# Taking GpSimd's elementwise work in the attention stage over to VectorE and ScalarE

## The chip, the cores and the metric

The kernel runs on one core of one Trainium2 chip. The metric is the device time of one execution in microseconds (us). Engines are named as in the profile: PE is TensorE's matmul and PEld its weight load, DVE is VectorE, ACT is ScalarE, POOL is GpSimd, SP is SyncE, which issues the DMAs.

## The reference: what is computed

One encoder block over 512 tokens plus 16 meta tokens, model width 1024, float32. All heads are 64 wide.

```
u = rms_norm(h, pre_mix_gain)
qa, ka, va, qb, kb, vb, g = split(u @ w_in)            # 1024 -> 6656 columns
qa, ka, qb, kb = rope(...)                             # x1*cos - x2*sin, x2*cos + x1*sin
o_swa  = softmax([q k^T in a window of 3 blocks, 16 meta keys, sink]) v     # 16 heads, 4 KV heads
o_diff = (softmax(q1 k1^T) - lam * softmax(q2 k2^T)) v                      # 8 heads, all 528 keys
o_diff = rms_norm(o_diff, per head) * (1 - lambda_init)
merged = sigmoid(g1 + b1) * (o_swa @ w_branch_swa) + sigmoid(g2 + b2) * (o_diff @ w_branch_diff)
h = h + rms_norm(merged @ w_out)
h = h + rms_norm((silu(a) * b) @ w_ffn_out),  [a, b] = rms_norm(h) @ w_ffn_in
```

## The kernel before

Every float32 operand of a large product is split into a high part (a rounded copy, written by ACT) and a low part (the source minus the high part, `sub_hi`). A product is then three matmuls, hi·hi, hi·lo and lo·hi, which `mm3` (L142 to L144) accumulates in PSUM. All weights come as tiles of 128x1024 float32: `load_w` issues the DMA on SP's queue, ACT writes the high part `wh` (L130), and `sub_hi` (L111) writes the low part `wl`. For the 48 weight tiles from the 4th to the 51st (a counter `nw`), POOL writes three quarters of `wl` (128x768) and DVE the last quarter (128x256); for the others DVE writes all of it.

The order of PE's instructions is fixed when the kernel is built: several streams, written as generators, are merged by a class `Order`, in which each stream states how much PE time it just used and how long its next operands will take (the table `LAT`). The streams are the two halves of windowed attention (`s_swa` for scores and softmax, `t_swa` for transposes and values), the same two of differential attention (`s_diff`, `t_diff`), and `fill`, which puts projections (`f_q`, `f_qk`, `f_vd`, `f_gate`, `f_b1` and others) between them. The order on DVE, ACT, POOL and SP's queue in this stage is chosen by the framework's scheduler, and each engine works its list strictly as it stands. An instruction with a wait holds up what is behind it on its engine.

The places that the change touches, in the order of the work:

- Rotary embedding (`rope`): DVE multiplies the two PSUM tiles by the cosines and sines (L325, L326) into `ta` and `tb`, POOL adds them (L327), ACT and DVE split the sum into `hl` (L118, L119). DMAs rearrange `hl` into the operands of the score products.
- Windowed attention works in 16 units (4 KV heads by 4 query blocks), each of four heads. Per head: two score matmuls into `Sw` (L465), DVE adds the mask and takes the smallest value (L468), ACT takes the exponential and its sum (L471). The sink value is put into the column behind the keys by a POOL copy of one column (L467). When all four sums are there, DVE inverts them (`rc`, L474) and POOL scales the four heads' rows (L476). Then PE transposes them (L516), ACT and DVE split the transposes into `ah` and `al` (L115, L111), and PE multiplies them with V (L530, L531, and L534 for the meta keys out of `aTm`).
- Differential attention: 8 heads of 4 query blocks, two softmaxes each. Per softmax four matmuls into `Sd` (L626), which is one buffer of two banks, a DVE minimum `dnm` (L629) and an ACT exponential (L630). Then DVE inverts the sums (L634), multiplies one by minus lambda (L635), POOL scales the first softmax (L636) and DVE adds the second (L638).
- Per head, the RMS norm over 128 rows of the output: ACT squares, `split(sh, sl, sq, eng=pool)` has POOL write the low part, PE sums (L691), ACT forms `v` and `y` = v^-0.5 (L695 to L697), and a Newton step follows: POOL computes z = y·y, z·v and 1.5 - 0.5·z (L699 to L701), DVE multiplies y by z (L702) and by gain and output (L703).

Of the kernel before, what the change touches and what calls it, by code (L numbers as in the profile page):

```python
"""Hybrid encoder block: windowed GQA with sink + differential attention, gated merge, SwiGLU FFN.

Every float32 operand of a large product is split exactly into two float32r parts (hi + lo);
a product is hi*hi + hi*lo + lo*hi accumulated in float32 in PSUM.
"""
# [10 lines left out]
AF = mybir.ActivationFunctionType  # L16
ALU = mybir.AluOpType
# [3 lines left out]
P = 128  # L21
# [13 lines left out]
class Order:  # L35
    """Order in which the tensor engine takes the work of several streams.

    A stream is a generator; it yields (cost, delay): the tensor time just traced and how long after
    it the stream's next piece has its operands, or a function that tells when (None: not yet) the
    next piece may follow. The first stream that is ready goes on."""  # L40
# [55 lines left out]
def encoder(ctx, tc, I, out, dbg=None):  # L96
# [25 lines left out]
    nw = [0]  # L122

    def load_w(src, k=KT, dst=None):
        raw = wp.tile([P, k, D // k], F32, tag="wr", name="wr", bufs=RB)
        sp.dma_start(out=raw, in_=src.rearrange("p (k c) -> p k c", k=k))
        if dst is None:
            dst = [wp.tile([P, k, D // k], F32R, tag=t, name=t) for t in ("wh", "wl")]
        wh, wl = dst
        act.copy(out=wh, in_=raw)  # L130
        # during attention the vector engine is the busiest: GpSimd takes three quarters of the low parts
        nw[0] += 1
        cut = 3 * k // 4 if 4 <= nw[0] < 52 else 0
        if cut:
            sub_hi(wl[:, 0:cut], raw[:, 0:cut], wh[:, 0:cut], pool)
        sub_hi(wl[:, cut:], raw[:, cut:], wh[:, cut:])
        return wh, wl
# [18 lines left out]
    def rsqrt_cols(pl, ss, n, scale, tag, extra=None, bufs=1):  # L156
        """(ss*scale + eps)^-0.5 on [n, m] columns, with one Newton step; extra replaces eps."""
# [54 lines left out]
    # the tensor engine's clock rises only under load  # L212
# [59 lines left out]
    # K of the windowed branch, slice by slice as x arrives; then V  # L272
# [13 lines left out]
    # row statistics of x: 1/rms, broadcast to all partitions  # L286
# [28 lines left out]
    # small vectors  # L315
# [5 lines left out]
    def rope(hl, psa, psb, c0, n, o0, scale=None):  # L321
        """psa, psb: [P, n] products of columns c0..c0+n; hl[:, part, hi/lo, o0..o0+n] gets the rotated split."""
# [4 lines left out]
        pool.tensor_tensor(out=ta, in0=ta, in1=tb, op=ALU.add)  # L327
# [104 lines left out]
    # per query block: (key column range, mask, [(offset in range, key block or -1 for meta)])  # L432
# [10 lines left out]
    # meta rows of the transposed probabilities; the gaps between the row groups stay zero  # L443
# [4 lines left out]
    def s_swa():  # L448
        for u in range(16):
# [9 lines left out]
            pt = atp.tile([P, 4, 401], F32, tag="p", name="p", bufs=2)  # L459
            for hh in range(4):  # L460
# [6 lines left out]
                pool.tensor_copy(out=p[:, nk:nk + 1], in_=nsink[:, h:h + 1])  # L467
# [7 lines left out]
            for hh in range(4):  # L475
                pool.tensor_scalar(out=pt[:, hh, 0:nk], in0=pt[:, hh, 0:nk], scalar1=rc[:, hh:hh + 1],  # L476
                                   scalar2=1.0, op0=ALU.mult, op1=ALU.mult)
# [5 lines left out]
    def pipe(n, tr_fn, av_fn, done_tr, free_at):  # L483
        """tr_fn(k), then av_fn(k, operand): two transposed banks ahead."""
# [122 lines left out]
    def s_diff():  # L607
        for h in range(8):
# [8 lines left out]
            for i in range(4):  # L617
# [4 lines left out]
                for c in range(2):  # L622
                    S = ps.tile([P, 2, 512], F32, tag="S", name="Sd")
                    for s in range(2):
                        for x in range(2):
# [10 lines left out]
                pool.tensor_scalar(out=pc[0], in0=pc[0], scalar1=rc[:, 0:1], scalar2=1.0,  # L636
                                   op0=ALU.mult, op1=ALU.mult)
# [7 lines left out]
    def t_diff():  # L645
        free_at = 0.0
        for h in range(8):
# [28 lines left out]
            # per-head RMS norm over the 128 rows of O  # L676
# [6 lines left out]
            split(sh, sl, sq, eng=pool)  # L683
# [15 lines left out]
            pool.tensor_tensor(out=z, in0=y, in1=y, op=ALU.mult)  # L699
            pool.tensor_tensor(out=z, in0=z, in1=v, op=ALU.mult)  # L700
            pool.tensor_scalar(out=z, in0=z, scalar1=-0.5, scalar2=1.5, op0=ALU.mult, op1=ALU.add)  # L701
            dve.tensor_tensor(out=y, in0=y, in1=z, op=ALU.mult)  # L702
# [14 lines left out]
    def f_tanh1():  # L717
        th = [act.activation(out=t1[:, j, :], in_=t1[:, j, :], func=AF.Tanh, scale=0.5, bias=hb[:, j:j + 1])
              for j in range(NB)]
        # one table set serves the Exp and the Ln of the differential branch  # L720
# [73 lines left out]
    # the eight banks as two sets of four  # L794
# [25 lines left out]
    # all of w_out stays on chip, in the space of the hidden activations  # L820
# [156 lines left out]
def _tiles(w, cols):  # L977
    """[1024, n] -> tiles of 128 columns (order given), each [128 rows-in-slice, slice*128 + col]."""
# [78 lines left out]
```

## Time and profile before

| what | value |
|---|---|
| median of 3 runs | 1016.48 us (1016.4 to 1017.12) |
| span of the profiled execution, first to last instruction | 1015.2 us |
| its own time less its span | not told; the runs are 1.2 to 1.9 us above the span |
| PE busy | 973.6 us, 96% of the span |
| PEld / DVE / ACT / POOL busy | 830.5 / 589.3 / 446.8 / 246.8 us |
| from the first 25 us to about 550 us | projections and attention |
| from about 550 us on | branch products, output projection, FFN |

The span is the time between the first and the last instruction that the profiler recorded. A busy share is a mean over stages; PE's is near its limit everywhere, so what can change is the time in which PE waits. Matmul records overlap, so PE can show busy while it is already late by a fraction of a matmul.

### The profile page before, as it was taken

To read this page: it belongs to the slowest core of one execution; us is meant where nothing else is said; L and a number is where in the kernel's file an instruction comes from. 1 tells how busy PE (TensorE), PEld (TensorE's weight loads), DVE (VectorE), ACT (ScalarE), POOL (GpSimd) and SP (SyncE) were. 2 spreads that over 40 slices of the span, in tenths; PEclk is the share of its full clock that TensorE was granted. 3 is DMA by queue.
4 is the path that set the end of the run, shared out by engine and by line. 5 is a ranking of instruction groups with operands and counts; after the bars stand their busy time and mean duration, and the time that the engine had idled before them with its cause. 6 is when DMAs were issued, how large, how long until landed. Compare 5 with 4: busy or idle time off the path is not lost.

```text
span 1015.2 us, 14301 instructions
## 1 busy us (share of the span) xinstructions
PE 973.6 (96%) x5355; PEld 830.5 (82%) x5355; DVE 589.3 (58%) x979; ACT 446.8 (44%) x820; POOL 246.8 (24%) x294
## 2 busy tenths in 40 slices
PE   9989999989999997998999999999999999999997
PEld 9767777869888887988887888998888888888885
DVE  5856788766675868788874574863333333322224
ACT  6336677565443654654556352543233233222121
POOL 1443454534434554543421000100000000000000
PEclk9998999999999999998999999999999999999999
DMA  9572131341515144233512471353323323324122
GB/s 329 157 196 71 43 83 43 92 117 46 146 61 147 43 126 123 57 100 100 145 59 90 134 230 56 112 175 104 102 86 104 102 84 104 102 86 145 57 68 83
DMA packets 36597, 109.33 MB, mean 108 GB/s; under 512 B 5921, under 2 KB 6433, under 8 KB 35889
## 3 DMA queue, kind: packets, MB, share of 16 engines
q1 hardware_dynamic: 36528, 108.42, 35.3%
q8 instruction: 42, 0.69, 0.3%
q14 instruction: 27, 0.21, 0.1%
HBM read 87.04 MB, written 2.10 MB: 88 GB/s over the span
## 4 chain that ended last, share of the span: by engine, by line
PE 73%; DVE 12%; DMA 4%; issue 4%; ACT 4%; POOL 2%; SPq 1%; DVEq 0%; ACTq 0%; POOLq 0%
PE pr L142 15%; PE pr L143 15%; PE pr L144 15%; PE wk L142 2%; PE wk L143 2%; PE wk L144 2%; PE tr L516 2%; DMA wr<-in_w_in_dram 2%; PE Sd L626 2%; DVE wl L111 2%; PE Sw L465 2%; PE acc L143 1%; PE tr L143 1%; PE acc L142 1%; PE tr L142 1%
## 5 line engine op out<-in xcount | busy, mean ns | idle before, releaser
L130 ACT CAST wh<-wr 128x1024 fp32r<-128x1024 f32 x134 | 140.7, 1051 | 279.1 <-PE pr L143 122.2
L111 DVE TENSOR_TENSOR wl<-wr,wh 128x1024 fp32r<-128x1024 f32 (+2 forms) x138 | 153.1, 1110 | 138.3 <-ACT wh L130 130.5
L142 PE MATMUL pr<-xh,wh 128*128 128x264 f32 (+1 forms) x616 | 199.9, 325 | 0.0
L143 PE MATMUL pr<-xl,wh 128*128 128x264 f32 (+1 forms) x616 | 197.7, 321 | 0.7 <-DVE xl L234 0.7
L144 PE MATMUL pr<-xh,wl 128*128 128x264 f32 (+1 forms) x616 | 197.4, 320 | 0.7 <-DVE wl L111 0.7
L144 PEld LDWEIGHTS pr<-xh,wl 128*128 128x128 f32 x616 | 117.0, 190 | 9.3 <-DVE wl L111 0.9
L143 PEld LDWEIGHTS pr<-xl,wh 128*128 128x128 f32 x616 | 117.2, 190 | 7.1 <-DVE xl L234 1.2
L142 PEld LDWEIGHTS pr<-xh,wh 128*128 128x128 f32 x616 | 117.1, 190 | 6.9 <-issue 1.2
L111 POOL TENSOR_TENSOR wl<-wr,wh 128x768 fp32r<-128x768 f32 x48 | 95.6, 1992 | 86.9 <-ACT wh L130 85.0
L142 PE MATMUL pr<-uh,wh 128*128 128x512 f32 (+1 forms) x304 | 110.8, 364 | 0.0
L143 PE MATMUL pr<-ul,wh 128*128 128x512 f32 (+1 forms) x304 | 110.6, 364 | 0.0
L144 PE MATMUL pr<-uh,wl 128*128 128x512 f32 (+1 forms) x304 | 110.6, 364 | 0.0
L164 POOL TENSOR_TENSOR r3y<-r3v,mhalf 128x1 f32<-128x1 f32 x4 | 2.2, 552 | 352.7 <-DVE r3v L163 352.7
L142 PEld LDWEIGHTS pr<-uh,wh 128*128 128x128 f32 x304 | 57.3, 189 | 9.1
L144 PEld LDWEIGHTS pr<-uh,wl 128*128 128x128 f32 x304 | 57.4, 189 | 9.1
L143 PEld LDWEIGHTS pr<-ul,wh 128*128 128x128 f32 x304 | 57.4, 189 | 9.0
L629 DVE TENSOR_REDUCE dnm<-Sd 128x1 f32<-128x528 f32 x64 | 44.9, 702 | 22.8 <-PE Sd L626 22.5
L626 PE MATMUL Sd<-Kd,Qd 128*128 128x264 f32 x256 | 44.4, 295 | 9.6 <-ACT pp L630 8.0
L471 ACT ACTIVATE p<-p,nm 128x273 f32<-128x273 f32 (+1 forms) x64 | 36.9, 576 | 30.9 <-DVE nm L468 21.9
L468 DVE CUSTOM_DVE_ANT_0 p<-Sw,mk,nsink 128x272 f32<-128x272 f32 (+1 forms) x64 | 36.0, 563 | 24.3 <-PE Sw L465 22.9
L327 POOL TENSOR_TENSOR ta<-ta,tb 128x528 f32<-128x528 f32 (+1 forms) x26 | 35.7, 1372 | 55.0 <-DVE tb L326 46.4
L626 PEld LDWEIGHTS Sd<-Kd,Qd 128*128 128x128 f32 x256 | 36.7, 191 | 14.4 <-ACT pp L630 11.4
(370 smaller groups left out, 1979.3 us busy)
## 6 DMA issues: line engine op xcount, KB each, us to landing
wr<-in_w_in_dram SPq DMA_DIRECT2D x50, 512.0 KB, 3.8
wr<-in_w_fi_dram SPq DMA_DIRECT2D x50, 512.0 KB, 3.5
wr<-in_w_fo_dram SPq DMA_DIRECT2D x22, 512.0 KB, 3.5
Kd<-hl SPq DMA_DIRECT2D x32, 132.0 KB, 2.4
Kd<-Kd SPq DMA_DIRECT2D x8, 528.0 KB, 4.3
Q<-hl SPq DMA_DIRECT2D x64, 64.0 KB, 2.0
Qd<-hl SPq DMA_DIRECT2D x64, 64.0 KB, 2.1
wr<-in_w_bs_dram SPq DMA_DIRECT2D x8, 512.0 KB, 3.5
```

The costliest lines, as they stand in the source:

```text
L111: (eng or dve).tensor_tensor(out=lo, in0=src, in1=hi.bitcast(F32), op=ALU.subtract)
L130: act.copy(out=wh, in_=raw)
L142: pe.matmul(out=ps, lhsT=ah, rhs=bh, start=first, stop=False)
L143: pe.matmul(out=ps, lhsT=ah, rhs=bl, start=False, stop=False)
L144: pe.matmul(out=ps, lhsT=al, rhs=bh, start=False, stop=last)
L327: pool.tensor_tensor(out=ta, in0=ta, in1=tb, op=ALU.add)
L465: pe.matmul(out=S, lhsT=Qs[g][hh // 2][:, hh % 2, i * P:(i + 1) * P], rhs=KK[g // 2][:, c, g % 2, r0:r1], start=(c == 0), stop=(c == 1))
L468: dve.tensor_tensor_reduce(out=p[:, 0:nk], in0=S, in1=mask, scale=1.0, scalar=nsink[:, h:h + 1], op0=ALU.add, op1=ALU.min, accum_out=nm[:, ...
L471: act.activation(out=p, in_=p, func=AF.Exp, scale=-1.0, bias=nm[:, hh:hh + 1], accum_out=den[:, hh:hh + 1])
L516: pe.transpose(out=tr[0:kk, hh * P:(hh + 1) * P], in_=pt[:, hh, o:o + kk], identity=ident)
L626: pe.matmul(out=S[:, s, 0:HALF], lhsT=Q[:, c, i * P:(i + 1) * P], rhs=K[:, x, c, s * HALF:(s + 1) * HALF], start=(x == 0), stop=(x == 1))
L629: dve.tensor_reduce(out=nm[:, c:c + 1], in_=S[:, :, 0:HALF], axis=AX.XY, op=ALU.min)
```

## The change

GpSimd's elementwise work in the attention stage goes to other engines. The low parts of all weight tiles are written whole by DVE; the rotary sum (L327) and the scaling of the first softmax (L636) go to DVE; the scaling of the four heads' rows (L476) goes to ACT; the low part of the squares goes to DVE; the Newton step becomes an ACT square and two fused DVE instructions. The 64 POOL copies of the sink become 16, one for each unit, ahead of the unit's matmuls. The order on PE and the table `LAT` stay as they are, and so do the DMAs. The diff also removes comments (left out here).

```diff
-        nw[0] += 1
-        cut = 3 * k // 4 if 4 <= nw[0] < 52 else 0
-        if cut:
-            sub_hi(wl[:, 0:cut], raw[:, 0:cut], wh[:, 0:cut], pool)
-        sub_hi(wl[:, cut:], raw[:, cut:], wh[:, cut:])
+        sub_hi(wl, raw, wh)
...
-        pool.tensor_tensor(out=ta, in0=ta, in1=tb, op=ALU.add)
+        dve.tensor_tensor(out=ta, in0=ta, in1=tb, op=ALU.add)
...
             pt = atp.tile([P, 4, 401], F32, tag="p", name="p", bufs=2)
+            pool.tensor_copy(out=pt[:, :, nk], in_=nsink[:, 4 * g:4 * g + 4])
             for hh in range(4):
...
-                pool.tensor_copy(out=p[:, nk:nk + 1], in_=nsink[:, h:h + 1])
...
             dve.reciprocal(out=rc, in_=den)
             for hh in range(4):
-                pool.tensor_scalar(out=pt[:, hh, 0:nk], in0=pt[:, hh, 0:nk], scalar1=rc[:, hh:hh + 1],
-                                   scalar2=1.0, op0=ALU.mult, op1=ALU.mult)
+                act.activation(out=pt[:, hh, 0:nk], in_=pt[:, hh, 0:nk], func=AF.Copy, scale=rc[:, hh:hh + 1])
...
-                pool.tensor_scalar(out=pc[0], in0=pc[0], scalar1=rc[:, 0:1], scalar2=1.0,
-                                   op0=ALU.mult, op1=ALU.mult)
+                dve.tensor_scalar(out=pc[0], in0=pc[0], scalar1=rc[:, 0:1], scalar2=None, op0=ALU.mult)
...
-            split(sh, sl, sq, eng=pool)
+            split(sh, sl, sq)
...
-            pool.tensor_tensor(out=z, in0=y, in1=y, op=ALU.mult)
-            pool.tensor_tensor(out=z, in0=z, in1=v, op=ALU.mult)
-            pool.tensor_scalar(out=z, in0=z, scalar1=-0.5, scalar2=1.5, op0=ALU.mult, op1=ALU.add)
-            dve.tensor_tensor(out=y, in0=y, in1=z, op=ALU.mult)
+            act.activation(out=z, in_=y, func=AF.Square)
+            dve.scalar_tensor_tensor(out=z, in0=z, scalar=-0.5, in1=v, op0=ALU.mult, op1=ALU.mult)
+            dve.scalar_tensor_tensor(out=y, in0=z, scalar=1.5, in1=y, op0=ALU.add, op1=ALU.mult)
```

## Rows read from the trace of the kernel before

**Rows 1.** Busy time of each engine in three stretches that make up most of attention (us; in brackets the number of instructions; PEclk is the granted clock of PE as a share of full speed, then the DMA engines' share and GB/s).

```profile
64.00:239.00 175.00, 163.56 (x894) 131.99 (x895) 128.58 (x292) 112.87 (x263) 80.02 (x141) 0.98 0.29 82
239.00:400.00 161.00, 152.48 (x1008) 136.82 (x1007) 115.66 (x176) 75.98 (x145) 76.05 (x55) 1.00 0.34 97
400.00:550.00 150.00, 141.45 (x906) 125.23 (x905) 110.32 (x177) 81.14 (x158) 56.80 (x47) 0.98 0.36 102
```

**Rows 2.** What PE waited for between 64 and 550 us, longest in total first (us in total, times, longest us).

```profile
PE Sd L626 <- ACT pp L630: 8.0, 7, 1.6
PE O L534 <- DVE aTm L111: 4.5, 3, 2.1
PE tr L658 <- DVE Vd L111: 3.5, 2, 2.0
PE Sw L465 <- DMA Q<-hl: 2.7, 1, 2.7
...
```

**Rows 3.** DVE's groups of instructions between 64 and 550 us, shapes apart (number, then busy us, mean ns of one, then idle time before them).

```profile
L111 DVE TENSOR_TENSOR wl<-wr,wh 128x256 fp32r<-128x256 f32 x42 | 37.2, 886 | 4.8 <-ACT wh L130 4.5 <-DMA Q<-hl 0.3
L638 DVE SCALAR_TENSOR_TENSOR pa<-pp,drc,pa 128x528 f32<-128x528 f32 x24 | 29.0, 1206 | 5.0 <-POOL pa L636 4.6
...
L119 DVE SCALAR_TENSOR_TENSOR hl<-ta,qsc,hl 128x528 fp32r<-128x528 f32 x16 | 17.7, 1107 | 2.3 <-ACT hl L118 2.2
L635 DVE TENSOR_TENSOR drc<-drc,nlam 128x1 f32<-128x1 f32 x32 | 17.1, 535 | 0.9
...
L545 DVE TENSOR_TENSOR of<-O,otmp 64x256 f32<-64x256 f32 x32 | 13.3, 416 | 9.8 <-ACT otmp L544 9.4
...
L111 DVE TENSOR_TENSOR dl<-ob,dh 128x512 fp32r<-128x512 f32 x7 | 6.8, 966 | 0.2
```

**Rows 4.** Two of these lines over the whole span (duration in ns: least, median, largest; start of the first and the last in us; shape).

```profile
L638 DVE SCALAR_TENSOR_TENSOR pa<-pp,drc,pa x24: 753/770/2352, 265.4 to 526.4; 128x528 f32<-128x528 f32 x24
L635 DVE TENSOR_TENSOR drc<-drc,nlam x32: 147/160/1329, 263.4 to 530.6; 128x1 f32<-128x1 f32 x32
```

**Rows 5.** Pieces of two stretches in order of time: start us, us, engine, line, operation (in square brackets the engine's idle time just before, and what ended it).

```profile
86.39 1.84 POOL L111 TENSOR_TENSOR wl<-wr,wh 128x768 fp32r<-128x768 f32 x1 [3.48 <-ACT wh L130]
86.49 2.02 DVE L111 TENSOR_TENSOR wl<-wr,wh 128x256 fp32r<-128x256 f32 x1
...
89.83 0.79 PE L534 MATMUL O<-aTm,Vm 48*128 48x512 f32 x1 [2.10 <-DVE aTm L111]
...
384.37 1.85 POOL L111 TENSOR_TENSOR wl<-wr,wh 128x768 fp32r<-128x768 f32 x1 [1.97 <-ACT wh L130]
384.42 2.35 DVE L111 TENSOR_TENSOR dl<-ob,dh 128x512 fp32r<-128x512 f32 x1
386.69 0.69 DVE L629 TENSOR_REDUCE dnm<-Sd 128x1 f32<-128x528 f32 x1
...
388.32 0.76 PE L626 MATMUL Sd<-Kd,Qd 128*128 128x264 f32 x4 [1.61 <-ACT pp L630]
```

**Rows 6.** Two stretches of 3 us that follow a wait of PE, columns as in rows 1.

```profile
90.00:93.00 3.00, 3.00 (x11) 2.26 (x12) 1.54 (x4) 0.59 (x1) 1.99 (x4) 0.50 0.37 152
464.00:467.00 3.00, 3.00 (x16) 3.00 (x15) 2.92 (x7) 0.20 (x1) 0.00 (x0) 0.50 0.68 125
```

**Rows 7.** POOL's groups between 64 and 550 us, columns as in rows 3.

```profile
L111 POOL TENSOR_TENSOR wl<-wr,wh 128x768 fp32r<-128x768 f32 x42 | 83.7, 1993 | 79.5 <-ACT wh L130 77.6 <-PE Sd L626 1.9
L327 POOL TENSOR_TENSOR ta<-ta,tb 128x528 f32<-128x528 f32 x16 | 22.7, 1420 | 39.1 <-DVE tb L326 33.5 <-DVE drc L634 5.6
L476 POOL TENSOR_SCALAR p<-p,rc 128x400 f32<-128x400 f32 x32 | 19.2, 619 | 16.0 <-DVE rc L474 16.0
```

**Rows 8.** DVE's durations where POOL has no such work: the whole weight tile (575 us to the end), and from the whole span a product of two SBUF operands in the first 64 us, a copy of one operand, and a product by a constant on one column; columns as in rows 3.

```profile
L111 DVE TENSOR_TENSOR wl<-wr,wh 128x1024 fp32r<-128x1024 f32 x72 | 88.2, 1224 | 124.3 <-ACT wh L130 121.3
...
L325 DVE TENSOR_TENSOR ta<-kraw,rot 128x528 f32<-128x528 f32 x2 | 1.4, 700 | 0.0
...
L306 DVE COPY rb<-r0y 128x128 f32<-128x128 f32 x4 | 0.6, 222 | 0.0
...
L165 DVE TENSOR_SCALAR r1h<-r1v 128x1 f32<-128x1 f32 x4 | 0.6, 152 | 0.1
```

**Rows 9.** ACT's groups between 64 and 239 us, columns as in rows 3.

```profile
L471 ACT ACTIVATE p<-p,nm 128x401 f32<-128x401 f32 x32 | 20.2, 630 | 12.5 <-DVE nm L468 8.9 <-POOL p L467 3.3
L471 ACT ACTIVATE p<-p,nm 128x273 f32<-128x273 f32 x32 | 16.7, 523 | 18.3 <-DVE nm L468 13.1 <-POOL p L467 4.0 <-POOL p L476 1.3
...
L721 ACT ACT_TABLE_LOAD x1 | 1.3, 1283 | 0.0
```

**Rows 10.** The end of one unit of windowed attention, in order of time, columns as in rows 5.

```profile
79.82 0.17 DVE L474 RECIPROCAL rc<-den 128x4 f32<-128x4 f32 x1
80.09 2.33 POOL L476 TENSOR_SCALAR p<-p,rc 128x400 f32<-128x400 f32 x4 [2.27 <-DVE rc L474]
80.35 0.59 ACT L115 CAST ah<-tr 128x512 fp32r<-128x512 f32 x1 [1.12 <-PE tr L516]
80.97 0.69 DVE L111 TENSOR_TENSOR al<-tr,ah 128x512 fp32r<-128x512 f32 x1 [0.98 <-ACT ah L115]
82.36 0.39 PE L530 MATMUL O<-ah,Vs 128*128 128x512 f32 x1
82.59 0.39 PE L531 MATMUL O<-al,Vs 128*128 128x512 f32 x1
```

More of the change, by code (lines that the diff above doesn't have):

```diff
@@ L120, in split @@
                                      op0=ALU.mult, op1=ALU.subtract)
-    nw = [0]
     def load_w(src, k=KT, dst=None):
```

## Prediction

> **What bounds the kernel now.** I read the page first: PE is busy 96% of the span, and no other engine comes near that. So only time in which PE stands, or runs at a lower clock, can go. The second view is the busy time by stretch, to find where PE stands [rows 1]. The reader subtracts PE's busy time from each stretch: 175 - 163.6 = 11.4, 161 - 152.5 = 8.5 and 150 - 141.5 = 8.5, together 28.5 us between 64 and 550 us. After 550 us PE stands only at the very end, where the change moves nothing. Attention is therefore the stage to read the change in, and 28.5 us is all the idle time that it can win there, beside the clock: the granted clock is 0.98 in the first and the third stretch, which is 0.02 x 175 + 0.02 x 150 = 6.5 us of full-speed time.
>
> The third view is PE's list of waits [rows 2]. Its first three lines, 8.0 + 4.5 + 3.5 = 16.0 us in twelve waits, are behind DVE or behind an ACT exponential that itself waits for DVE's minimum. The DMA wait of 2.7 us lies ahead of the stretches.
>
> The fourth view shows why DVE is late: its groups by shape [rows 3] and the spread of two lines [rows 4]. The addition of the second softmax (L638) takes 0.77 us at the median and 2.35 at most; the product on one single column (L635) 0.16 and 1.33. The work is the same each time, so something holds it. The order of time shows what [rows 5]: at 384.4 us DVE starts the low part `dl` within 0.05 us of a POOL weight low part of 1.85 us and needs 2.35 us for 512 columns; the minimum behind it on DVE starts at 386.7, and PE stands 1.61 us. At 86.5 us the quarter tile takes DVE 2.02 us beside a POOL piece of 1.84 us, and PE stands 2.10 us for `aTm`. A DVE instruction with one operand in PSUM is not touched: L545 stays at 416 ns over 32 instructions [rows 3]. POOL's two-operand work thus costs DVE time, which is the fact that decides how I cost the change.
>
> **What the change removes.** Let me call the time above the undisturbed duration the stretch, and count it between 64 and 550 us [rows 3, 4]. Quarter tiles: 37.2 - 42 x 0.416 = 19.7 us (0.416 is L545, as many columns). L638 on `pa`: 29.0 - 24 x 0.77 = 10.5. `hl`, as long as L638: 17.7 - 16 x 0.77 = 5.4. L635: 17.1 - 32 x 0.16 = 12.0. `dl`: 6.8 - 7 x 0.70 = 1.9. Together 49.5 us of DVE's 354.6 [rows 1]. All of it should go, since nothing on POOL is left there but 16 copies of a few columns.
>
> **What it adds to DVE.** A whole weight tile takes 1.224 us [rows 8], so the 42 quarters grow by 42 x (1.224 - 0.416) = 33.9 us. The rotary sum is a product or sum of two SBUF operands, 0.70 [rows 8]: 16 of 528 columns [rows 7] and the eight shorter ones of the windowed queries (four groups by two halves), at most 24 x 0.70 = 16.8. The scaling of the first softmax is an operation with one tensor operand on DVE, which the trace does not show at this size. It lies between a copy of 128 columns, 0.22, and L638's two operands on 528 columns, 0.77, so 32 of them cost 7.1 to 24.6. I take the line through one column (0.152) and 128 columns (0.222) [rows 8]: 0.152 + 527 x 0.00055 = 0.44, that is 14.1. [...] The low part of the squares is 8 x 0.70 = 5.6, and the Newton step has one DVE instruction more per head, 5.6. Sum 76.0. Net of the stretch DVE gains 26.5 us of work: 354.6 becomes 381 of 486 us, 78% where it was 73%. It is not the bound. But its longest instruction falls from 2.35 to 1.22 us.
>
> **What it adds to ACT.** The 64 scalings: nearest are ACT's exponentials over the same rows, 0.630 and 0.523 [rows 9], so 32 x 0.630 + 32 x 0.523 = 36.9 us, all in the first stretch, where ACT goes from 112.9 to 149.8 of 175 us, 86%. [...] POOL needs 0.619 for the 400-column scaling [rows 7], so the step itself becomes no shorter by the move: it only changes the queue in which it stands. Copies with a scale already run between the exponentials (L118), and that stretch has a single table load [rows 9], so I count none. The eight squares add some 0.6 us each on an ACT that has room after 239 us: nothing.
>
> **What that is on PE's path.**
> - The twelve large waits. In the two shown places [rows 5] the 2.02 us tile becomes 1.22, so 0.80 of 2.10 goes; `dl` falls by 1.65, so all of the 1.61 goes: 2.41 of 3.71, or 65%. On 16.0 us this is -10.4. Bounds: nothing, and all 28.5.
> - The clock. Two stretches at 0.50 follow waits of PE [rows 6], worth 6.5 us together. I take half, -3.2, since shorter waits may or may not be short enough. Bounds 0 and -6.5.
> - ACT's queue. In the unit shown [rows 10] the inverse is there at 79.99 us. Four scalings of 0.63 on ACT would hold it to about 82.5, while `ah` now starts at 80.35. It would end at 83.1, against L530 at 82.36, and `al` at 83.8 against L531 at 82.59: about 1.2 us late. That needs a transpose to fall into the 2.5 us, and the scheduler to let the scalings go first. I take a quarter of 16 units: +5. Bounds 0 and 16 x 1.2 = +19.
> - DVE's 26.5 us of new work, in pieces of at most 0.8. PE now stands 28.5 us for 354.6 of DVE's, 0.08 per us: +2. With the share that I gave the stretch, 10.4 / 49.5 = 0.21, it would be +6.
> - At nothing: the shorter chains of rotary sum, softmax scaling and Newton step. The projections on PE cover them, and the fixed order of PE does not use what comes early. If that cover is gone, the rotary sum is worth 1.42 - 0.70 us per projection. The single sink copy per unit: POOL is empty by then. No DMA moves.
>
> Sum: -10.4 - 3.2 + 5 + 2 = -6.6. Span 1015.2 - 6.6 = 1008.6; the median of the runs lies 1.3 above the span, so 1009.9 us, with a range of its own of 1003 to 1014.
>
> **The rivals.**
> - ACT's queue eats the gain (slower). For: 86% on a queue that serves `ah`, `aTm` and the exponentials, all of which PE waits for within a microsecond or two. Against: ACT has 62 us of idle time there [rows 1], and after the inverse shown it served nothing for 0.36 us, and only 0.59 us of `ah` next [rows 10]. It decides from the point where eleven of the 16 units lose 1.2 us (13.6 - 2 = 11.6 us to be used up, less than 11 x 1.2 = 13). If all do: 1015.2 - 11.6 + 19 + 1.3 = 1024. [...] Chance 0.20.
> - DVE becomes the bound of differential attention (slower): the whole tiles stand where the quarters stood, in front of the minimum that frees `Sd`. If the net 26.5 us reached PE at 0.8 a microsecond, +21 in place of +2 would give 1029; at half of that 1018. Against: 78% on average. Chance 0.06.
> - The waits only move (no change). The two engines' order is chosen anew by the scheduler; with a third of the first term (-3.5), no clock and +4 from the rest the time stays at 1015 to 1018. Chance 0.14.
> - More comes back than I count: all 16.0 us of the first three lines and both clock spells, with nothing lost on ACT: 1015.2 - 22.5 + 1.3 = 994. Chance 0.12.
>
> **How the numbers follow.** The forecast has 0.48. Faster by over 0.2% (2 us, about what a measurement of this kernel tells from no change) is 0.48 + 0.12 = 0.60, no change 0.14, slower 0.20 + 0.06 = 0.26. The range goes from 995, inside the last rival, to 1026, past the ACT case with all units late; some 0.1 to 0.15 lies outside.
>
> **What the profile after would show.** L638, `hl` and L635 back at 0.77, 0.77 and 0.16 us at the mean, and no DVE instruction of the stage over 1.3 us: the stretch is gone. `wl` at 1.224 us everywhere. The scaling on DVE at 0.44, on ACT at 0.63 and 0.52. PE's waits for `pp`, `aTm` and `Vd` together near 6 us in place of 16.0. Granted clock above 0.98 in at least one of the two stretches. ACT near 86% between 64 and 239 us, with new PE waits for `ah` of about 5 us. The prediction is wrong if PE's waits for `ah` and `al` in that stretch pass 13 us, if `Sd` still waits 8 us with undisturbed DVE durations, or if the stretch stays although POOL is empty, which would mean that POOL was not its cause.

## The result, and the profile after

The change makes the kernel slower: 1020.74 us (1019.09 to 1022.83) against 1016.72 us (1014.67 to 1018.9) for the kernel before, eight runs of each, a ratio of 1.0037 [1.0024, 1.0049]. The profiled run has a span of 1019.4 us against 1015.2, so 4.2 us have to be found.

Three marks that both kernels have cut the span into stages: the inversion of the sums `rc` (once for each of the 16 units of windowed attention), PE's sum of the squares `mp` (once for each differential head), and the last product of the branch with `dh`. The view is that of one tile's instructions, one line from each of three: duration in ns (smallest, median, largest), then the start of the first and of the last in us. Before:

```profile
L474 DVE RECIPROCAL rc<-den x16: 164/168/180, 72.2 to 230.4; 128x4 f32<-128x4 f32 x16
L691 PE MATMUL mp<-sl,ones x8: 392/397/501, 326.6 to 548.8; 128*128 128x512 f32 x8
L144 PE MATMUL pr<-dh,wl x64: 389/389/389, 557.2 to 600.1; 128*128 128x512 f32 x64
```

After:

```profile
L467 DVE RECIPROCAL rc<-den x16: 167/171/178, 70.2 to 233.1; 128x4 f32<-128x4 f32 x16
L682 PE MATMUL mp<-sl,ones x8: 390/397/398, 329.8 to 549.4; 128*128 128x512 f32 x8
L137 PE MATMUL pr<-dh,wl x64: 388/389/628, 557.7 to 604.3; 128*128 128x512 f32 x64
```

Up to the first `rc`: 72.2 before, 70.2 after, -2.0. Windowed attention, first to last `rc`: 230.4 - 72.2 = 158.2 and 162.9, +4.7. Differential attention, up to the last `mp`: 318.4 and 316.3, -2.1. The tail, up to the last `dh` product: 51.3 and 54.9, +3.6. From there to the end both take 415.1. The sum is +4.2: two places win some 2 us each, two lose more, and the last of them lies behind attention, where I had looked for nothing.

Busy time by stretch of after, which answers to [rows 1] (PE, PEld, DVE, ACT, POOL, then the granted clock):

```profile
64.00:239.00 175.00, 159.72 (x852) 128.27 (x852) 126.57 (x291) 137.42 (x320) 3.56 (x14) 0.96 0.28 78
239.00:400.00 161.00, 156.92 (x1051) 141.79 (x1050) 121.67 (x211) 80.60 (x155) 0.00 (x0) 1.00 0.38 105
400.00:550.00 150.00, 138.54 (x893) 122.61 (x893) 117.07 (x206) 82.84 (x162) 0.00 (x0) 0.99 0.35 94
```

In the first stretch PE now stands 175 - 159.7 = 15.3 us (11.4 before) and its granted clock went down to 0.96 (0.98 before). DVE does 126.6 + 121.7 + 117.1 = 365.3 us of work in the three stretches, 10.7 more than before.

DVE's groups between 64 and 550 us, shapes apart, answer to [rows 3, 4]:

```profile
L111 DVE TENSOR_TENSOR wl<-wr,wh 128x1024 fp32r<-128x1024 f32 x50 | 61.0, 1220 | 4.3 <-ACT wh L128 4.1
...
L629 DVE SCALAR_TENSOR_TENSOR pa<-pp,drc,pa 128x528 f32<-128x528 f32 x24 | 18.3, 762 | 0.3
...
L628 DVE TENSOR_SCALAR pa<-pa,drc 128x528 f32<-128x528 f32 x24 | 11.7, 487 | 0.0
L320 DVE TENSOR_TENSOR ta<-ta,tb 128x528 f32<-128x528 f32 x16 | 11.3, 705 | 0.3
...
L627 DVE TENSOR_TENSOR drc<-drc,nlam 128x1 f32<-128x1 f32 x32 | 5.0, 155 | 0.6
```

The stretch, in the prediction's sense of time above an instruction's undisturbed duration, is gone, as forecast: the second softmax takes 762 ns in place of 1206, the one column 155 in place of 535. PE's waits over the same time answer to [rows 2] (us in total, times, longest):

```profile
PE Sd L618 <- ACT pp L622: 5.8, 5, 1.9
PE O L526 <- DVE aTm L111: 5.0, 4, 1.5
PE O L522 <- DVE of L537: 4.0, 1, 4.0
PE tr L649 <- DVE pp L629: 3.1, 2, 1.8
...
```

DVE's instructions are no longer held, yet PE's waits behind DVE, or behind an exponential that waits for DVE's minimum, are nearly as long as they were: 5.8 + 5.0 + 3.1 = 13.9 us for `pp`, `aTm` and the transposes, where the three first lines of [rows 2] had 16.0. New are single waits of 4.0 us (`of`) and 2.7 us (`al`, shown below) and, further down the list, 2.8 us for an `aTm` of differential attention, which was 0.2 before.

### The profile page after: what moved, and what is told of

The parts are those of the page before. It is cut to its first block, busy times and chain, and to the rows that moved or that the text cites. A ratio compares the mean times of both kernels' runs of the same rounds, so it can differ in the third digit from the quotient of the medians.

```text
span 1019.4 us, 13995 instructions
## 1 busy us (share of the span) xinstructions
PE 976.3 (96%) x5355; PEld 833.1 (82%) x5355; DVE 601.6 (59%) x1053; ACT 478.6 (47%) x892; POOL 14.2 (1%) x44
## 4 chain that ended last, share of the span: by engine, by line
PE 74%; DVE 13%; ACT 5%; DMA 4%; issue 2%; SPq 2%; DVEq 0%; ACTq 0%
PE pr L135 16%; PE pr L136 16%; PE pr L137 16%; PE wk L135 2%; PE wk L136 2%; PE wk L137 2%; DVE wl L111 2%; PE Sd L618 2%; PE tr L508 2%; PE Sw L459 2%; PE acc L137 1%; PE tr L137 1%; PE acc L135 1%; PE tr L135 1%; PE acc L136 1%
## 5 line engine op out<-in xcount | busy, mean ns | idle before, releaser
L111 DVE TENSOR_TENSOR wl<-wr,wh 128x1024 fp32r<-128x1024 f32 (+1 forms) x138 | 166.4, 1206 | 139.0 <-ACT wh L128 131.3
L622 ACT ACTIVATE pp<-Sd,dnm 128x528 f32<-128x528 f32 x40 | 27.9, 696 | 21.5 <-DVE dnm L621 21.2
L459 PE MATMUL Sw<-KK,Q 128*128 128x272 f32 (+1 forms) x128 | 32.8, 338 | 3.4 <-DMA Q<-hl 2.8
L135 PE MATMUL wk<-uh,wh 128*128 128x512 f32 (+1 forms) x96 | 34.8, 362 | 0.0
```

Source lines behind the costliest of these rows:

```text
L111: (eng or dve).tensor_tensor(out=lo, in0=src, in1=hi.bitcast(F32), op=ALU.subtract)
L135: pe.matmul(out=ps, lhsT=ah, rhs=bh, start=first, stop=False)
L459: pe.matmul(out=S, lhsT=Qs[g][hh // 2][:, hh % 2, i * P:(i + 1) * P], rhs=KK[g // 2][:, c, g % 2, r0:r1], start=(c == 0), stop=(c == 1))
L622: act.activation(out=p.rearrange("p (a b) -> p a b", a=2), in_=S[:, :, 0:HALF], func=AF.Exp, scale=-1.0, bias=nm[:, c:c + 1], accum_out=de ...
```

## The experiments

All stand against the kernel before, whose median was 1016.7 to 1017.6 us beside them. The stages are taken by the three marks from one profiled run of each kernel. The runs of one kernel lie up to 5.6 us apart, so a difference of a microsecond or two between the stages of two profiles shows little unless other versions repeat it.

| kernel | median, us | ratio [95%] | to first `rc` | windowed | differential | tail |
|---|---|---|---|---|---|---|
| before | 1016.72 | 1 | 72.2 | 158.2 | 318.4 | 51.3 |
| after | 1020.74 | 1.0037 [1.0024, 1.0049] | 70.2 | 162.9 | 316.3 | 54.9 |
| scalings_back | 1010.18 | 0.9934 [0.9914, 0.9954] | 71.1 | 154.7 | 315.4 | 55.0 |
| scalings_act_only | 1029.70 | 1.0130 [1.0109, 1.0151] | 71.7 | 167.5 | 321.9 | 51.3 |
| scalings_dve | 1019.98 | 1.0039 [1.0025, 1.0054] | 69.9 | 162.5 | 316.1 | 53.3 |
| half_on_act | 1019.99 | 1.0030 [1.0017, 1.0043] | 70.8 | 158.6 | 318.2 | 51.3 |
| no_scalings | 1010.49 | 0.9946 [0.9927, 0.9964] | 70.8 | 154.7 | 315.8 | 54.9 |
| square_on_dve | 1018.26 | 1.0017 [1.0005, 1.0030] | 70.0 | 161.8 | 318.0 | 51.2 |
| back_and_square | 1010.06 | 0.9937 [0.9922, 0.9951] | 70.0 | 154.7 | 317.9 | 51.2 |
| square_before_sigmoids | 1007.65 | 0.9909 [0.9891, 0.9927] | 70.1 | 154.9 | 314.9 | 51.2 |
| no_softmax_scaling | 1004.44 | 0.9882 [0.9859, 0.9905] | 70.3 | 155.0 | 312.2 | 53.4 |
| tiles_dve_only | 1010.20 | 0.9940 [0.9923, 0.9957] | 71.1 | 153.9 | 317.0 | 51.3 |
| mixed | 1010.72 | 0.9943 [0.9927, 0.9959] | 71.1 | 153.9 | 317.9 | 51.2 |
| tiles_and_sums | 1005.71 | 0.9887 [0.9868, 0.9905] | 71.0 | 153.4 | 313.0 | 51.2 |

### Is it the four scalings on ACT?

scalings_back is the changed kernel with the windowed scalings on POOL again; scalings_act_only is the kernel before with nothing but those scalings and the sink copy changed.

```diff
             for hh in range(4):
-                act.activation(out=pt[:, hh, 0:nk], in_=pt[:, hh, 0:nk], func=AF.Copy, scale=rc[:, hh:hh + 1])
+                pool.tensor_scalar(out=pt[:, hh, 0:nk], in0=pt[:, hh, 0:nk], scalar1=rc[:, hh:hh + 1],
+                                   scalar2=1.0, op0=ALU.mult, op1=ALU.mult)
```

> The changed kernel with one part undone: the scaling of the four heads' rows in windowed attention is on POOL again (the sink is still copied once per unit). Theory A, ACT's queue: the 64 scalings on ACT push casts that PE waits for, most of the loss lies there. Then PE's idle time between 64 and 239 us falls from 15.3 to about 10 us, its clock there back to 0.98 or more, and the time is 1012 to 1016 us. Theory B, DVE's whole tiles: what DVE took over costs as much as the stretch gave back and ACT is no matter; the time stays at 1019 to 1022 us. Theory C, the order: any edit lets the scheduler deal DVE's and ACT's work anew and the places of the waits change by chance; anything from 1012 to 1022, with the large waits at new places.

> The kernel before with one part of the change alone: the scaling of the four heads' rows on ACT, with one sink copy per unit; POOL keeps the low parts, the rotary sums and the rest. Theory A: slower than before by 5 to 9 us, 1022 to 1026, PE's idle time between 64 and 239 us at 15 us or more, the other two stretches as before. Theory B: 1015 to 1018, no change, since DVE's work is the same. Theory C: within 4 us of before either way, with the large waits at new places.

Measured: back on POOL, the kernel comes to 1010.18 us, 10.6 below the changed one and 6.5 below the one before, more than theory A had expected. On ACT alone they add 13, where theory A had 5 to 9: 9.3 in windowed attention, and 3.5 in differential attention, where it had expected no change. There PE spends 13.7 us at half its clock in place of 6.8, which is 3.4 us lost; what set these spells off isn't shown. The inversions of scalings_back, and its first stretch:

```profile
L474 DVE RECIPROCAL rc<-den x16: 161/171/179, 71.1 to 225.8; 128x4 f32<-128x4 f32 x16
```

```profile
64.00:239.00 175.00, 165.57 (x921) 133.74 (x920) 131.19 (x301) 114.40 (x267) 38.40 (x78) 0.99 0.29 82
```

Windowed attention takes 225.8 - 71.1 = 154.7 us in place of 162.9: 8.2 us for this one edit. PE stands 9.4 us in the stretch in place of 15.3, and its granted clock is 0.99 in place of 0.96. Between the marks, where PE does the same products, it stands 13.3 us with the scalings on ACT and 8.5 on POOL, and is busy for 149.6 and 146.2 us: 4.8 of the 8.2 us are waiting, and in 3.4 PE is busy longer, at the lower clock. The order of time in the changed kernel shows how it costs (start, duration; in brackets the idle time before, and what ended it):

```profile
210.17 0.17 DVE L467 RECIPROCAL rc<-den 128x4 f32<-128x4 f32 x1
210.37 2.19 ACT L469 ACTIVATE p<-p,rc 128x400 f32<-128x400 f32 x4 [1.64 <-DVE rc L467]
...
212.46 0.56 ACT L115 CAST ah<-tr 128x512 fp32r<-128x512 f32 x1
...
213.05 0.69 DVE L111 TENSOR_TENSOR al<-tr,ah 128x512 fp32r<-128x512 f32 x1 [2.72 <-ACT ah L115]
...
213.80 0.38 PE L362 MATMUL tr<-ident,VT 128*16 128x128 f32 x1 [2.70 <-DVE al L111]
```

The same place in the kernel before:

```profile
210.22 2.33 POOL L476 TENSOR_SCALAR p<-p,rc 128x400 f32<-128x400 f32 x4 [1.90 <-DVE rc L474]
...
210.49 0.59 ACT L115 CAST ah<-tr 128x512 fp32r<-128x512 f32 x1 [2.38 <-PE tr L516]
...
211.85 0.28 PE L369 MATMUL tr<-ident,VT 128*16 128x128 f32 x1 [0.96 <-DVE al L111]
```

ACT takes the four scalings in one block of 2.19 us, no longer than POOL's 2.33, but `ah`, which belongs to the unit before, stands behind it: it starts at 212.46 in place of 210.49, and PE stands 2.70 us in place of 0.96. The block was uninterrupted in all 16 units (1.76 us with 272 columns, up to 2.2 with 400): in none of them does a cast pass it. The longest new wait, 4.0 us for `of` at 177.47, is in part the same at second hand: behind a block that starts at 168.34 ACT works without a pause until 175.5, and the copy `otmp` that `of` needs comes to its turn at 173.99. It is done at 174.36, but on DVE `of` then stands until 176.91 behind a whole weight tile, two `al` and a rotary sum, so DVE's own queue, with work taken over from POOL, has its share in that wait. PE kept its order in that wait: a projection of which nine products ran from 172.24 on, and whose weight tile was complete at 162.64, goes on only behind it, at 180.88.

### Is it ACT's load, or any queue that PE waits for?

scalings_dve has the scalings on DVE, half_on_act (out of the kernel before) has heads 0 and 2 on ACT and 1 and 3 on POOL, and no_scalings is scalings_back with the scalings left out.

```diff
+                dve.tensor_scalar(out=pt[:, hh, 0:nk], in0=pt[:, hh, 0:nk], scalar1=rc[:, hh:hh + 1], scalar2=None, op0=ALU.mult)
...
+                if hh % 2 == 0: act.activation(out=pt[:, hh, 0:nk], in_=pt[:, hh, 0:nk], func=AF.Copy, scale=rc[:, hh:hh + 1])
+                else: pool.tensor_scalar(out=pt[:, hh, 0:nk], in0=pt[:, hh, 0:nk], scalar1=rc[:, hh:hh + 1], scalar2=1.0, op0=ALU.mult, op1=ALU.mult)
```

> The changed kernel with the scaling of the four heads' rows on DVE in place of ACT (some 0.37 and 0.31 us each by the changed kernel's 0.487 for 528 columns, so four make 1.2 to 1.5 us). If any in-order queue that PE waits for suffers from the scalings, this costs 3 to 8 us over the version with POOL (1010.2), so 1013 to 1018; if it is ACT's queue alone, 1009 to 1012.

> The kernel before with the scaling of two of each unit's four heads on ACT and of the other two on POOL (one sink copy per unit); all else as before. All four on ACT cost 12 us. Theory L, load: what counts is the sum of ACT's work, and half of it costs half, 1022 to 1025 us. Theory K, the block: what counts is that four scalings in a row (1.8 to 2.2 us) keep a cast from PE longer than the microsecond or so that it has to spare, and a block of two (0.9 to 1.1 us) mostly fits; 1016 to 1020 us, and PE's waits behind al, aTm and of between 64 and 239 us near those of before.

> The version with the scalings of windowed attention on POOL, with these 64 scalings left out (their rows go on undivided; nothing else is left out). If POOL did them wholly beside PE's path, leaving them out brings nothing: 153 to 156 us from the first to the last inverse of windowed attention (154.7 with POOL, 162.9 with ACT, 162.5 with DVE), 1008 to 1011 us. If the chain through them mattered, 150 or less and 1003 to 1006.

On DVE the windowed stage is 162.5 us, as on ACT (162.9), although ACT is relieved; 1019.98 us is more than the 1013 to 1018 expected. The place where it costs in scalings_dve:

```profile
131.63 1.44 DVE L476 TENSOR_SCALAR p<-p,rc 128x400 f32<-128x400 f32 x4
...
132.98 0.49 DVE L468 CUSTOM_DVE_ANT_0 p<-Sw,mk,nsink 128x272 f32<-128x272 f32 x1
...
133.54 0.51 PE L465 MATMUL Sw<-KK,Q 128*128 128x272 f32 x2 [1.36 <-DVE nm L468]
```

Now it is the minimum, which frees `Sw`, that stands behind the block, and PE waits 1.36 us. The 8 us are made up otherwise than on ACT: PE stands 15.3 us between the marks, at a granted clock of 1.00. With the scalings left out the stage is 154.7 us, exactly what it is with them on POOL. So POOL does them for nothing and either of the two busy engines charges about 8 us. What counts is the queue: POOL's holds nothing that PE needs soon. The chance of the order, theory C, doesn't account for it: the eight versions with whole weight tiles on DVE and the scalings on POOL or left out lie at 153.4 to 155.0 us in this stage, the three with the scalings on ACT or DVE at 161.8 to 162.9.

Half the block shows that the loss isn't proportional to the work: half_on_act has 158.6 us in the windowed stage against 158.2, and a ratio of 1.0030 [1.0017, 1.0043] where the whole block has 1.0130 [1.0109, 1.0151]. Its runs lie far apart (1016.1 to 1021.4, and the profiled one, with a span of 1014.0, is the fastest), so what half a block costs stays open; that it is less than half of the whole doesn't.

### What costs 3.6 us behind attention?

The tail of the changed kernel, ACT's instructions and PE's product that waits for them:

```profile
551.17 0.63 ACT L688 ACTIVATE y<-y 128x512 f32<-128x512 f32 x1
551.82 1.28 ACT L770 ACT_TABLE_LOAD   x1
553.12 3.79 ACT L770 ACTIVATE z<-z,hb 128x512 f32<-128x512 f32 x6
556.81 1.03 ACT L128 CAST wh<-wr 128x1024 fp32r<-128x1024 f32 x1
557.75 0.63 ACT L690 ACTIVATE z<-y 128x512 f32<-128x512 f32 x1
...
562.86 0.62 ACT L115 CAST dh<-ob 128x512 fp32r<-128x512 f32 x1 [2.30 <-DVE ob L693]
...
563.52 0.49 PE L135 MATMUL pr<-dh,wh 128*128 128x512 f32 x1 [1.33 <-ACT dh L115]
```

For the last head `y` is ready at 551.80. Its square, now an ACT instruction, stands behind the table load, six sigmoids of the gates and a weight cast, and starts at 557.75; before, POOL took it at 551.43 with nothing ahead of it. Behind the square, DVE puts a weight tile and a gate product ahead of z·v and another tile ahead of `y`. `dh` starts at 562.86 in place of 558.86, PE stands 1.33 us, and 1.7 us later its clock is halved:

```profile
565.50:568.50 3.00, 3.00 (x9) 2.32 (x8) 2.63 (x4) 0.96 (x2) 0.00 (x0) 0.50 0.01 3
```

The spell lasts 565.2 to 568.7, half of which is lost: 1.33 + 1.7 = 3.0 of the 3.6 us. The table has the two parts: scalings_dve and no_softmax_scaling have the same late square and the same wait of 1.3 us, but no spell follows it (granted clock 1.00), and their tails are 53.3 and 53.4 us in place of 54.9 and 55.0. To show that the square is the cause, square_on_dve has it on DVE in the changed kernel, back_and_square in scalings_back; square_before_sigmoids (from scalings_back) leaves it on ACT and puts it on the list `lnx` of instructions that the sigmoids have to follow.

```diff
-            act.activation(out=z, in_=y, func=AF.Square)
+            dve.tensor_tensor(out=z, in0=y, in1=y, op=ALU.mult)
...
+            lnx.append(act.activation(out=z, in_=y, func=AF.Square))
```

> The changed kernel with the square of the Newton step on DVE in place of ACT. In the changed kernel PE waits 1.3 us for the last head's dh at 562 us and its clock is halved for 3.4 us after that. Theory: the last square stands behind the sigmoid's activations on ACT; on DVE it does not, the wait and the spell go and the time falls by 1.3 + 1.7, to 1017 to 1019 us. If the wait comes from the longer list of DVE instead, the time stays at 1020 to 1022 us.

> The changed kernel with the two undone parts together: scalings of windowed attention on POOL, square of the Newton step on DVE. If the two losses are separate, the gains add: 1020.7 less 10.6 less 2.5, that is 1007 to 1009 us. If both come from one lack of time on ACT, the second brings nothing more: 1010 to 1011.

> The changed kernel with the scalings of windowed attention back on POOL, and with the order on ACT fixed in one place: the sigmoid's activations of the differential branch may start only behind the last square. In the changed kernel that square waits from 551.8 to 557.8 us behind a table load, six sigmoid activations and a weight cast. Theory: this is the whole of the loss at the end of attention (the stretch from the last sum of squares to the last product with dh lasts 54.9 us and 51.3 in the kernel before), and it goes without moving work to DVE: 51 to 52 us for that stretch, 1006 to 1009 for the kernel. If the loss is DVE's longer list, that stretch stays at 54 to 55 and the time at 1010.

The tail is back at 51.2 us in all three, so DVE's longer list alone does not make the loss. In square_before_sigmoids:

```profile
543.12 0.63 ACT L699 ACTIVATE z<-y 128x512 f32<-128x512 f32 x1
...
545.06 4.40 ACT L780 ACTIVATE z<-z,hb 128x512 f32<-128x512 f32 x7
```

But back_and_square missed: it wins the tail (55.0 to 51.2) and loses 2.5 us in differential attention (315.4 to 317.9), so that its median is that of scalings_back. The reordered square keeps both, 1007.65 us. That the eight squares, 8 x 0.68 = 5.5 us of DVE, cost 2.5 us there is a difference of two profiles: 1.1 us of it are waiting, and 1.4 are PE at work longer for the same products, with a spell at half clock of 6.8 us in place of 3.4. With the scalings on ACT the same edit lengthens that stage by 1.7 us (316.3 to 318.0). The direction repeats, the size isn't settled.

### Where did DVE's gain go in differential attention?

One place in back_and_square shows DVE's queue without any stretch:

```profile
447.72 0.68 DVE L701 SCALAR_TENSOR_TENSOR y<-z,y 128x512 f32<-128x512 f32 x1
...
448.32 0.76 DVE L119 SCALAR_TENSOR_TENSOR hl<-ta,qsc,hl 128x528 fp32r<-128x528 f32 x1
...
449.00 0.42 DVE L363 TENSOR_TENSOR VT<-pr,rbc 128x264 f32<-128x264 f32 x1
...
449.35 0.69 DVE L629 TENSOR_REDUCE dnm<-Sd 128x1 f32<-128x528 f32 x1
...
449.94 1.04 ACT L130 CAST wh<-wr 128x1024 fp32r<-128x1024 f32 x1 [2.91 <-PE pr L143]
...
450.89 0.69 ACT L630 ACTIVATE pp<-Sd,dnm 128x528 f32<-128x528 f32 x1
...
451.73 0.75 PE L626 MATMUL Sd<-Kd,Qd 128*128 128x264 f32 x4 [1.71 <-ACT pp L630]
```

The `Sd` that `dnm` reads is complete at 447.83. Three DVE instructions at their undisturbed durations, the last link of the Newton step among them, keep the minimum from it for 1.5 us, and a weight cast on ACT then keeps the exponential back for another 0.85; PE's next `Sd` product starts at 451.73 after 1.71 us of waiting. no_softmax_scaling takes the scaling of the first softmax (L636) out of scalings_back altogether.

```diff
-                dve.tensor_scalar(out=pc[0], in0=pc[0], scalar1=rc[:, 0:1], scalar2=None, op0=ALU.mult)
```

> The version with the scalings of windowed attention on POOL, with the 32 scalings of the first softmax on DVE (L636, 0.49 us each, 15.6 us) left out (the first softmax goes on undivided; nothing else is left out). Theory: in differential attention PE waits for the minimum that stands behind a backlog of DVE's own work, which took the place of the time that POOL held DVE; 16 us less of it shortens the stretch from the last inverse of windowed attention to the last sum of squares (315.4 us) by 3 us or more. If DVE's load is not what those waits depend on, the stretch stays within 1.5 us.

Without these 32 x 0.487 = 15.6 us of DVE the stage falls from 315.4 to 312.2: 3.2 us, or 0.2 per us of DVE, and the kernel to 1004.44 (1.6 us of that is the tail without its spell). But the gain isn't where the theory put it. PE's waits in the stage, scalings_back and then no_softmax_scaling:

```profile
PE Sd L626 <- ACT pp L630: 5.8, 5, 1.9
PE tr L658 <- DVE pp L638: 3.1, 2, 1.8
```

```profile
PE Sd L626 <- ACT pp L630: 5.3, 5, 1.7
...
PE tr L658 <- DVE pp L638: 1.1, 2, 0.8
```

The wait behind the minimum loses 0.5 us, the wait of the transposes for the second softmax 2.0, and the scaling that was left out is a link of the chain to that second softmax. So a shorter chain explains the gain as well as a shorter queue on DVE does; no run here separates them.

The last three runs give DVE parts of POOL's work alone, out of the kernel before: tiles_dve_only the whole weight tiles, mixed the tiles, the first softmax's scaling and the low part of the squares, tiles_and_sums the tiles, the rotary sums and the low part of the squares.

```diff
-        cut = 3 * k // 4 if 4 <= nw[0] < 52 else 0
+        cut = 0
...
-        pool.tensor_tensor(out=ta, in0=ta, in1=tb, op=ALU.add)
+        dve.tensor_tensor(out=ta, in0=ta, in1=tb, op=ALU.add)
...
-            split(sh, sl, sq, eng=pool)
+            split(sh, sl, sq)
```

> The kernel before with one part of the change alone: DVE writes the low parts of all weight tiles whole, POOL keeps sums, scalings and the Newton step. Theory B: this is the larger part of the net work on DVE and it costs 2 to 5 us, 1018 to 1022. Theory A: the largest piece of POOL's contention goes (about 96 of its 247 us of busy time) and ACT is as before, so the time is 1010 to 1015. Theory C: within 4 us of before either way.

> The kernel before with three parts of the change: whole low parts of weights, scaling of the first softmax and low part of the squares on DVE; POOL keeps the rotary sums, the scalings of windowed attention and the Newton step. Against the version that moves only the low parts of the weights (1010.2): the scaling of the first softmax leaves DVE no longer waiting for POOL in L638 and L635, so 1006 to 1010 if that stretch mattered; 1010 to 1013 if DVE's own work takes its place.

> The kernel before with three parts of the change: whole low parts of the weights, rotary sums and low part of the squares on DVE; POOL keeps both kinds of scaling and the Newton step. Nothing is moved to ACT. 1007 to 1011 us; near 1010 again if, below POOL's weight low parts, it makes no difference who adds and scales; under 1008 if the sum on POOL still held DVE.

The tiles alone win 6.5 us, all of what scalings_back wins. Adding the softmax scaling and the squares wins nothing (1010.72 against 1010.20); adding the rotary sums and the squares wins 4.5 more, past the 1007 to 1011 expected, and the two intervals don't touch. tiles_and_sums is the fastest complete kernel here, 1005.71 us (1004.54 to 1005.87), 15 below the changed one and 11 below the one before. It leaves with POOL what has one tensor operand or runs once per head. What this costs DVE shows in the second softmax of tiles_and_sums (smallest, median, largest duration in ns), and at one of its long instances in order of time:

```profile
L638 DVE SCALAR_TENSOR_TENSOR pa<-pp,drc,pa x24: 751/766/1792, 258.8 to 515.3; 128x528 f32<-128x528 f32 x24
```

```profile
508.25 1.29 POOL L700 TENSOR_TENSOR z<-z,v 128x512 f32<-128x512 f32 x1
...
508.32 1.79 DVE L638 SCALAR_TENSOR_TENSOR pa<-pp,drc,pa 128x528 f32<-128x528 f32 x1 [0.71 <-POOL pa L636]
```

The mean is 876 ns, beside 762 with POOL idle and 1206 before, but it is a mean of two kinds: 21 of the 24 take 751 to 775 ns, three of these beside POOL's scaling of `z` by a constant, and the other three, 1.53 to 1.79 us, lie beside z·v, a two-operand product of the Newton step. What the rotary sums on POOL cost shows elsewhere, in the whole weight tiles of tiles_dve_only, which take 1314 ns in the mean where those of the changed kernel take 1220 and those of tiles_and_sums 1228:

```profile
L111 DVE TENSOR_TENSOR wl<-wr,wh 128x1024 fp32r<-128x1024 f32 x50 | 65.7, 1314 | 5.2 <-ACT wh L130 5.1
```

```profile
244.07 1.32 POOL L327 TENSOR_TENSOR ta<-ta,tb 128x528 f32<-128x528 f32 x1 [4.53 <-DVE tb L326]
...
244.24 2.23 DVE L111 TENSOR_TENSOR wl<-wr,wh 128x1024 fp32r<-128x1024 f32 x1 [0.26 <-ACT wh L130]
```

## Why the prediction was wrong

I forecast a span of 1008.6; it is 1019.4, 10.8 us more. square_before_sigmoids splits the miss, since it is the changed kernel without its two losses: its span is 1006.2, and its stages differ from those of the changed kernel by 8.0 us (windowed), 1.4 (differential), 3.7 (tail) and 0.1.

- **The waits and the clock, -10.4 - 3.2, with DVE's new work at +2: -11.6 in all.** The runs give -9.0 (1015.2 to 1006.2): -2.1 up to the first `rc`, -3.3 in windowed, -3.5 in differential attention, nothing in the tail. The clock came as forecast: two spells at half clock of 6.8 us each have become two of 3.4, and PE is busy 3.2 us less for the same products. Waiting fell by 5.8 and not by 8.4. The step that failed here is the 65% that I took from two shown places and applied to all twelve waits: those three lines go from 16.0 us to 5.9 + 3.1 + 3.1 = 12.1 in square_before_sigmoids, 3.9 in place of 10.4, and 1.8 us of the gain lie ahead of the first `rc`, where I had counted nothing. That POOL's two-operand work held DVE was right, and tiles_dve_only shows that POOL's weight low parts alone were worth 6.5 us. What the waits still stand behind is DVE's own list and ACT's, as at 449 us. DVE's new work was not measured by itself: at the 0.2 us per us of no_softmax_scaling, 10.7 us of net work make the +2 that I had, though I had it from 26.5 us at 0.08, which is luck.
- **ACT's queue, +5, bounds 0 and 19.** Measured by scalings_back, +8.2 in the stage (8.0 against square_before_sigmoids), and 10.6 between the medians. The mechanism was named and the term too small by 3. The price of one instruction was right:

```profile
L469 ACT ACTIVATE p<-p,rc 128x400 f32<-128x400 f32 x32 | 17.5, 621 | 2.4 <-DVE rc L467 2.4
...
L469 ACT ACTIVATE p<-p,rc 128x272 f32<-128x272 f32 x32 | 14.1, 511 | 0.9 <-DVE rc L467 0.9
```

  0.621 and 0.511 where I took 0.630 and 0.523 from [rows 9]. Wrong was the quarter of the units: in all 16 the scalings ran as one block ahead of whatever came next. They become ready together, and what became ready a moment later waited for the rest of the block, which takes 1.76 to 2.20 us. I had weighed that by a chance, and here it held each time. Wrong on the other side were the 1.2 us for each unit: 8.2 us over 16 units are 0.5, much of it in a few long waits. Nor did I price the clock here: I let half of its loss come back, and in this stretch the loss doubled, from 0.02 to 0.04 of 175 us (3.5 us more). The rival of ACT's queue, at 0.20, came nearest to what happened, but by its own condition, 11.6 us to be used up, the 8.2 would not have made the kernel slower; square_on_dve, which has them without the tail's loss, is at 1.0017 of the kernel before.
- **"At nothing: the shorter chains of ... Newton step".** This step failed outright, +3.6. I looked at how long the chain is and not at the queue into which its first link moved: a chain of 1.04 + 1.30 + 0.62 us on an engine with nothing else to do became shorter in work, but its first link started 6.3 us later (551.43 and 557.75), once per kernel, in front of the product that PE needed next. For the square I wrote that ACT has room after 239 us. Room is an average; at 551.8 us there was none. And "After 550 us PE stands only at the very end, where the change moves nothing" overlooked that the last head's norm falls there. No rival named this.
- **The rest, 1.4 us in differential attention,** is between the changed kernel and square_before_sigmoids and not settled; scalings_back alone accounts for 0.9 of it.
- **Right:** the end of the stretch and its cause, the price of the whole tile (1.220 for 1.224) and of the rotary sum (0.705 for 0.70). DVE's net work grew by less than forecast, 10.7 and not 26.5 us. Part of that is stretch on lines that I had not listed, as 2.6 us on the addition on `pp`; part is the counting, since the busy times of DVE's groups grow by 17 us in sum, and the busy time of the stretch counts pieces that overlap once. DVE didn't become a bound over the stage; it did in places.

So of the 10.8 us, 2.6 are the gain, 3.0 ACT's queue, 3.7 the tail, 1.4 differential attention and 0.1 the rest.

None of the three signs of being wrong came: the stretch went, `Sd` waits 5.8 us and not 8, and of the other signs two misled me. The waits for `ah` and `al` in the first stretch are 0.2 + 2.7 + 1.4 = 4.3 us, near the 5 forecast and far from 13: most of what ACT's queue cost stands under other names, 5.0 us for `aTm` and 4.0 for `of`, and in the clock. ACT is at 137.4 of 175 us, 79% and not 86%. The sign that spoke is the sum of the three old lines, 13.9 where I had set 6.

## What to carry to other kernels

Before work is moved off a slow engine, look at what stands behind it in the new queue, not at how busy the new engine is: here a block of four scalings that became ready at one moment held up what PE waited for next, 8.2 us in the windowed stage with the block on ACT, and the side engine on which nobody waited did the same work for nothing, 154.7 us with the scalings on POOL and with them left out. Take from the side engine only what disturbs the others (here its two-operand work beside DVE, 1206 ns in place of 762 for the second softmax), and leave with it what doesn't. For a chain that is "covered", check the last time it runs as well as the typical one: the cover may be missing there, and instructions of another phase may already be in the queue.

## What the runs showed of the hardware that I had not expected

The scaling on DVE took 0.487 us for 528 columns, and 1.44 us for four of 400. The line through a 1-column and a 128-column copy had given 0.44.

POOL's work with one tensor operand held DVE far less than its two-operand work. In tiles_and_sums, where POOL keeps both kinds, the second softmax takes 767 to 775 ns beside a POOL instruction with one operand alone and 1.53 to 1.79 us beside z·v, with 762 ns undisturbed. In scalings_back, where POOL has the windowed scalings and no two-operand work between 64 and 550 us, the whole weight tile takes 1221 ns in the mean, and 1220 in the changed kernel; `hl` of 512 columns takes 700 and 684.

After a short wait of PE more time was lost than the wait lasted. The 1.33 us for `dh` were followed, 1.7 us after their end, by 3.4 us at a granted clock of 0.50, in which PE starts a 512-column product every 0.43 us, and every 0.23 after it; wait and spell together cost 3.0 us, more than twice the wait. That the wait sets the spell off is not shown: in scalings_dve the same wait is followed by a granted clock of 1.00, and in its stretch from 64 to 239 us PE stands 16.2 us, in waits of up to 1.7 us, at a granted clock of 1.00. Such spells came four more times in the changed kernel within attention, three of them in the windowed stage; between 214 and 217 us the granted clock is 0.50. PE's granted clock was 1.00 before, from 208 to 211 us, and this spell begins at 213.7, where the wait of 2.70 us that was shown above ends.
